# Batched matrix product on one core: loads by groups of four batches, row tiles, and the transposition of x on VectorE

## The chip, the cores and the metric

The kernel runs on one core of a Trainium2 chip. Its time is device microseconds for one launch, here the median of three runs. The profile beside it is one execution of the same program. Five engines work in parallel, each through its own list of instructions in order: TensorE (PE, with its weight loads listed as PEld), VectorE (DVE), ScalarE (ACT), GpSimd (POOL) and SyncE (SP). SP issues the transfers (DMAs) between HBM and the on-chip memory SBUF; 16 DMA engines carry them out. TensorE writes its products to PSUM, a memory of 8 banks, and VectorE or ScalarE copies them from there to SBUF.

## What is computed

```python
batch, dim_i, dim_j, dim_k = 32, 256, 512, 384
# x: (32, 256, 512) float32, y: (32, 512, 384) float32
def reference(x, y):
    return np.einsum('bij,bjk->bik', x, y).astype(np.float32)
```

These are 32 independent products of a 256 x 512 matrix with a 512 x 384 matrix. x is 16.8 MB, y 25.2 MB, the result 12.6 MB: 54.5 MB in all. TensorE needs the summed index j on the partitions for both operands. y has it there as it lies; x must be transposed. Both kernels round x and y to float16 before the products.

## The kernel before

**Tiles.** P is 128, the number of partitions. x is loaded for a group of Q = 4 batches at once (L63): 32 partitions belong to each batch and each holds 8 whole rows of x, 16 KB in one piece. y is loaded for each batch (L69): partition q holds the 4 rows of y with j = 4q to 4q + 3, 6 KB in one piece. The result of a batch is stored (L135) with two rows of 384 on each partition, 3 KB in one piece.

**Steps of the work on one group or batch.** `transpose(q)` turns the x of a group on TensorE: 32 transposes of 128 x 128 float32 elements against an identity matrix (L84), four to a PSUM bank; each full bank is copied out by VectorE (L92) or ScalarE (L94) in turn, rounded to float16 and written with a step of four elements, so that the rows of a batch stand in the order in which they are wanted. `round_y(b)` casts the four 384-element parts of a batch's y, two on ScalarE (L102) and two on VectorE (L104). `multiply(b)` makes the product of a batch from 8 matmuls (L115): four slices t of j, two halves e of the result's rows, each with 128 rows to sum over and 384 columns, gathered in two PSUM banks. `collect(b)` copies the two banks to SBUF, one on ScalarE (L128), one on VectorE (L130).

**Order.** The order on each engine is the order of the program (`keep`). The loop runs over batches s from 0 to B + 1 (L141 on): load the y of batch s + 6 and, with the first batch of a group, its x; collect batch s - 2; multiply batch s - 1; transpose the group if s begins one; round the y of batch s; store batch s - 2. All transfers are issued by SP, in this order, and an instruction that waits on SP holds back all behind it. The buffers: three groups of x, ten batches of y, four of rounded y, two groups of transposed x, ten batches of results, four PSUM banks for the transposes and four for the products. Beside what a transfer waits for by its buffers, it waits until the eighth one before it on SP has landed, as eight semaphores are used in turn; this holds for both kernels.

Of the kernel before, what the change touches and what calls it, by code (L numbers as in the profile page):

```python
# [1 line left out]

# [5 lines left out]


MM_DT = mybir.dt.float16  # L10
F32 = mybir.dt.float32
P = 128


Q = 4

LAG = 8

ON_ACT = ()


@with_exitstack
def kernel(
    ctx: ExitStack,
    tc: tile.TileContext,
    x: bass.AP,
    y: bass.AP,
    out: bass.AP,
):
    nc = tc.nc  # L30

    B, I, J = x.shape
    _, _, K = y.shape

    NI = I // P
    NJ = J // P


    R = Q * NI
    PQ = P // Q  # L40

    const_pool = ctx.enter_context(tc.tile_pool(name="const", bufs=1))
    x_pool = ctx.enter_context(tc.tile_pool(name="x_pool", bufs=3))
    y_pool = ctx.enter_context(tc.tile_pool(name="y_pool", bufs=10))
    yr_pool = ctx.enter_context(tc.tile_pool(name="yr_pool", bufs=4))
    xt_pool = ctx.enter_context(tc.tile_pool(name="xt_pool", bufs=2))
    o_pool = ctx.enter_context(tc.tile_pool(name="o_pool", bufs=10))
    tpsum_pool = ctx.enter_context(tc.tile_pool(name="tpsum", bufs=4, space=bass.MemoryType.PSUM))
    opsum_pool = ctx.enter_context(tc.tile_pool(name="opsum", bufs=4, space=bass.MemoryType.PSUM))


    keep = tc.keep_in_program_order

    identity = const_pool.tile([P, P], F32)
    make_identity(nc, identity)

    x_of, y_of, yr_of, xt_of, ps_of, o_of = {}, {}, {}, {}, {}, {}

    def load(b):
        if b % Q == 0:  # L60
            x_of[b // Q] = x_pool.tile([P, R, J], F32, name="x_sb")
            keep(
                nc.sync.dma_start(  # L63
                    out=x_of[b // Q],
                    in_=x[b : b + Q].rearrange("g (p r) j -> (g p) r j", r=R),
                )
            )
        y_of[b] = y_pool.tile([P, NJ, K], F32, name="y_sb")
        keep(nc.sync.dma_start(out=y_of[b], in_=y[b].rearrange("(q t) k -> q t k", q=P)))  # L69

    def transpose(q):

        x_sb = x_of.pop(q)
        xt_of[q] = xt_pool.tile([P, Q, NJ, NI, PQ, Q], MM_DT, name="xt_sb")
        n = 0
        for t in range(NJ):
            for e in range(NI):  # L80
                t_ps = tpsum_pool.tile([P, Q, Q, PQ], F32, name="t_ps")
                for h in range(Q):
                    keep(
                        nc.tensor.transpose(  # L84
                            t_ps[:, h].rearrange("c g p -> c (g p)"),
                            x_sb[:, h * NI + e, t::NJ],
                            identity,
                        )
                    )
                dst = xt_of[q][:, :, t, e].rearrange("c g p h -> c h g p")  # L90
                if n % 2 == 0:
                    keep(nc.vector.tensor_copy(dst, t_ps))  # L92
                else:
                    keep(nc.scalar.copy(dst, t_ps))  # L94
                n += 1

    def round_y(b):
        y_sb = y_of.pop(b)
        yr_of[b] = yr_pool.tile([P, NJ, K], MM_DT, name="y_r")
        for t in range(NJ):  # L100
            if t % 2 == 0:
                keep(nc.scalar.copy(yr_of[b][:, t], y_sb[:, t]))  # L102
            else:
                keep(nc.vector.tensor_copy(yr_of[b][:, t], y_sb[:, t]))  # L104

    def multiply(b):
        xt_sb, y_r = xt_of[b // Q][:, b % Q], yr_of.pop(b)
        ps_of[b] = [
            opsum_pool.tile([P, K], F32, name=f"o_ps_{e}", tag="o_ps")
            for e in range(NI)  # L110
        ]
        for t in range(NJ):
            for e in range(NI):
                keep(
                    nc.tensor.matmul(  # L115
                        ps_of[b][e],
                        xt_sb[:, t, e].rearrange("c p h -> c (p h)"),
                        y_r[:, t],
                        start=(t == 0),
                        stop=(t == NJ - 1),  # L120
                    )
                )

    def collect(b):
        o_of[b] = o_pool.tile([P, NI, K], F32, name="o_sb")
        for e in range(NI):
            if e % 2 == 0:
                keep(nc.scalar.copy(o_of[b][:, e], ps_of[b][e]))  # L128
            else:
                keep(nc.vector.tensor_copy(o_of[b][:, e], ps_of[b][e]))  # L130
        del ps_of[b]

    def store(b):
        eng = nc.scalar if b in ON_ACT else nc.sync
        keep(eng.dma_start(out=out[b].rearrange("(m e) k -> m e k", m=P), in_=o_of.pop(b)))  # L135


    ahead = LAG - 2
    for b in range(ahead):
        load(b)  # L140
    for s in range(B + 2):  # L141
        if s + ahead < B:
            load(s + ahead)
        if s >= 2:
            collect(s - 2)
        if 1 <= s <= B:
            multiply(s - 1)
        if s < B and s % Q == 0:
            transpose(s // Q)
        if s < B:  # L150
            round_y(s)
        if s >= 2:
            store(s - 2)


# [1 line left out]
_INS = ['x', 'y']  # L157
_OUTS = [((32, 256, 384), 'float32')]


# [23 lines left out]
```

## Time and profile before

| | |
|---|---|
| time, median of 3 runs | 136.32 us (136.06 to 136.57) |
| the profiled execution | 136.52 us |
| its span, first instruction to last | 134.7 us |
| mean granted clock of TensorE in it | 0.887 of full speed |
| read from HBM, written to it | 41.94 MB, 12.58 MB |
| mean rate over the span | 405 GB/s |
| first x landed, first transpose | 8.69 us |
| last eviction (L130) begins | 129.00 us |

The profile page counts the busy time of each engine, cuts the span into 40 slices and gives for each the busy tenths of every engine and of the DMA engines, follows back the chain of work that ended last, and lists groups of like instructions with the time of one and the idle time before them. A group's row reads: line, engine, operation, output and inputs with their shapes, count; busy time in us and the mean of one in ns; the idle time before them and what ended it. Busy shares are means over the whole span, and an engine's idle time costs nothing if it isn't on that chain.

### The profile page before, as it was taken

How to read it: one execution, taken by the hardware profiler on the slowest of the kernel's cores; microseconds unless marked ns; L12 is line 12 of the kernel's file. 1: busy time of each engine (PE TensorE's matmuls, PEld its weight loads, DVE VectorE, ACT ScalarE, POOL GpSimd, SP SyncE). 2: the span in 40 equal slices, each digit the busy share in tenths (PEclk: the TensorE clock that was granted, in tenths of full speed). 3: DMA queues.
4: the chain of work that ended last, by engine and by line, in shares of the span. 5: the costliest groups of instructions: out<-in, count | busy, mean ns of one | idle time of the engine just before them, and what ended most of it. 6: DMA issues, size and time to landing. Idle time of an engine off the chain costs nothing.

```text
span 134.7 us, 1539 instructions
## 1 busy us (share of the span) xinstructions
PE 89.5 (66%) x512; PEld 66.6 (49%) x512; DVE 73.7 (55%) x128; ACT 80.1 (59%) x129; POOL 0.7 (1%) x6
## 2 busy tenths in 40 slices
PE   0049499769677908949794983949459492794920
PEld 0048368644564408925492543936259360793510
DVE  0008855975397503873489340796228870378720
ACT  3007994996299602795479650699218990179910
POOL 2000000000000000000000000000000000000000
PEclk9999999999999985686999599599995999559995
DMA  5999999999999999999999999999999999999992
GB/s 131 399 413 423 447 412 416 416 434 414 404 422 451 425 399 424 421 435 437 400 416 430 438 425 410 421 418 454 407 409 425 433 440 402 421 421 413 412 410 84
DMA packets 10375, 54.62 MB, mean 405 GB/s; under 512 B 1152, under 2 KB 1152, under 8 KB 9344
## 3 DMA queue, kind: packets, MB, share of 16 engines
q1 hardware_dynamic: 10368, 54.53, 97.9%
q8 instruction: 4, 0.07, 0.2%
q14 instruction: 3, 0.02, 0.0%
HBM read 41.94 MB, written 12.58 MB: 405 GB/s over the span
## 4 chain that ended last, share of the span: by engine, by line
DMA 79%; PE 8%; ACT 5%; DVE 2%; issue 2%; SPq 1%; DVEq 0%
DMA y_sb<-in_y_dram 30%; DMA x_sb<-in_x_dram 27%; DMA out_dram<-o_sb 21%; PE o_ps L115 4%; PE t_ps L84 4%; ACT xt_sb L94 2%; ACT y_r L102 2%; DVE xt_sb L92 1%; DVE y_r L104 1%; DVE o_sb L130 0%; SPq L69 0%; ACT o_sb L128 0%; SPq L63 0%; DVEq L130 0%
## 5 line engine op out<-in xcount | busy, mean ns | idle before, releaser
L94 ACT CAST xt_sb<-t_ps 128x512 f16<-128x512 f32 x32 | 39.8, 1350 | 44.0 <-PE t_ps L84 43.9
L92 DVE CAST xt_sb<-t_ps 128x512 f16<-128x512 f32 x32 | 40.1, 1323 | 40.3 <-PE t_ps L84 40.2
L84 PE MATMUL t_ps<-identity,x_sb 128*128 128x128 f32 x256 | 43.4, 340 | 24.5 <-DMA x_sb<-in_x_dram 24.3
L115 PE MATMUL o_ps<-y_r,xt_sb 128*128 128x384 f16 x256 | 46.3, 342 | 14.9 <-ACT y_r L102 14.9
L84 PEld LDWEIGHTS t_ps<-identity,x_sb 128*128 128x128 f32 x256 | 41.1, 216 | 27.8 <-issue 26.4
L115 PEld LDWEIGHTS <-xt_sb 128*128 128x128 f16 x256 | 26.2, 102 | 34.2 <-issue 19.9
L102 ACT CAST y_r<-y_sb 128x384 f16<-128x384 f32 x64 | 30.2, 527 | 0.6 <-DMA y_sb<-in_y_dram 0.6
L130 DVE COPY o_sb<-o_ps 128x384 f32<-128x384 f32 x32 | 17.8, 556 | 15.1 <-PE o_ps L115 15.1
L104 DVE CAST y_r<-y_sb 128x384 f16<-128x384 f32 x64 | 19.9, 354 | 0.4 <-DMA y_sb<-in_y_dram 0.4
L128 ACT COPY o_sb<-o_ps 128x384 f32<-128x384 f32 x32 | 15.4, 483 | 3.8 <-PE o_ps L115 3.8
L94 ACT ACT_TABLE_LOAD x1 | 1.3, 1283 | 0.7 <-PEq L168 0.7
masks.py:199 POOL TENSOR_SCALAR_AFFINE_SELECT identity<-identity 128x128 f32<-128x128 f32 x1 | 0.3, 294 | 0.1
masks.py:197 POOL MEMSET identity<- 128x128 f32 x1 | 0.2, 205 | 0.3 <-POOLq L168 0.3
L168 POOL MEMSET const-bfloat16-1.0<- 128x1 bf16 x1 | 0.1, 102 | 0.0
L168 POOL MEMSET const-uint8-127<- 128x1 uint8 x1 | 0.1, 102 | 0.0
L168 POOL MEMSET const-float32-0.0<- 128x1 f32 x1 | 0.1, 99 | 0.2 <-issue 0.2
L168 POOL MEMSET const-float32-1.0<- 128x1 f32 x1 | 0.1, 99 | 0.0
## 6 DMA issues: line engine op xcount, KB each, us to landing
y_sb<-in_y_dram SPq DMA_DIRECT2D x32, 768.0 KB, 15.1
x_sb<-in_x_dram SPq DMA_DIRECT2D x8, 2048.0 KB, 14.2
out_dram<-o_sb SPq DMA_DIRECT2D x32, 384.0 KB, 14.1
```

The costliest lines, as they stand in the source:

```text
L84: nc.tensor.transpose(t_ps[:, h].rearrange("c g p -> c (g p)"), x_sb[:, h * NI + e, t::NJ], identity,)
L92: keep(nc.vector.tensor_copy(dst, t_ps))
L94: keep(nc.scalar.copy(dst, t_ps))
L102: keep(nc.scalar.copy(yr_of[b][:, t], y_sb[:, t]))
L104: keep(nc.vector.tensor_copy(yr_of[b][:, t], y_sb[:, t]))
L115: nc.tensor.matmul(ps_of[b][e], xt_sb[:, t, e].rearrange("c p h -> c (p h)"), y_r[:, t], start=(t == 0), stop=(t == NJ - 1),)
L128: keep(nc.scalar.copy(o_of[b][:, e], ps_of[b][e]))
L130: keep(nc.vector.tensor_copy(o_of[b][:, e], ps_of[b][e]))
L168: nc = _bacc.Bacc("TRN2", target_bir_lowering=False, num_devices=1)
```

## The change

The kernel now works on groups of four batches throughout, with 32 partitions to each batch in x and in y.

- **Loads.** x as before, one transfer for a group, but into two buffers instead of three. y is loaded for a group too: each of the 32 partitions of a batch holds 16 rows of y, 24 KB in one piece (two buffers). Only the last group's y comes in two halves of 12 KB.
- **Transposition of x.** TensorE no longer transposes and the identity matrix is gone. ScalarE copies x, rounded to float16, into a buffer `xr` so that two rows of x stand side by side as one 4-byte word; it reads with a step of 16 elements and writes with a step of two. VectorE then transposes blocks of 32 x 32 such words within each group of 32 partitions and writes the words with a step of two. A group takes four copies of 1024 elements and four transposes of 512 words.
- **Products.** Each matmul sums over 32 rows instead of 128. The four batches of a group take the four row tiles of TensorE (partitions 0 to 31, 32 to 63 and so on), one after the other in the program. A group has 16 x 2 x 4 = 128 matmuls of 384 columns into all eight PSUM banks.
- **Rounding of y.** Eight parts of 768 elements in a group: five on VectorE and three on ScalarE (`ROUND`).
- **Order.** In step n: load the x of group n + 2 and the y of group n + 1, round y and multiply group n, transpose the x of group n + 1, collect group n, store group n - 1. The last step stores group 7.

The core of the diff:

```diff
+LATE = 8
+LAST = 2
+ROUND = (1, 0, 1, 1, 0, 1, 0, 1)
...
+    S = P // Q
+    R = I // S
+    C = J // S
...
+    NE = I // P
+    A = R // NE // 2
+    N = B // Q
...
+    x_pool = ctx.enter_context(tc.tile_pool(name="x_pool", bufs=2))
+    xr_pool = ctx.enter_context(tc.tile_pool(name="xr_pool", bufs=1))
     xt_pool = ctx.enter_context(tc.tile_pool(name="xt_pool", bufs=2))
+    y_pool = ctx.enter_context(tc.tile_pool(name="y_pool", bufs=2))
+    yr_pool = ctx.enter_context(tc.tile_pool(name="yr_pool", bufs=2))
+    o_pool = ctx.enter_context(tc.tile_pool(name="o_pool", bufs=12))
+    psum_pool = ctx.enter_context(tc.tile_pool(name="psum", bufs=Q * NE, space=bass.MemoryType.PSUM))
...
+    def load_y(n):
+        y_of[n] = y_pool.tile([P, C, K], F32, name="y_sb")
+        src = y[n * Q : (n + 1) * Q].rearrange("g (p c) k -> (g p) c k", c=C)
+        w = C // (LAST if n == N - 1 else 1)
+        for c in range(0, C, w):
+            keep(nc.sync.dma_start(out=y_of[n][:, c : c + w], in_=src[:, c : c + w]))
...
+    def transpose_x(n):
+        x_sb = x_of.pop(n)
+        xr = xr_pool.tile([P, A, NE, C, S], F32, name="x_r")
+        xt = xt_pool.tile([P, C, NE, S, A], F32, name="xt_sb")
+        for a in range(A):
+            for e in range(NE):
+                keep(
+                    nc.scalar.copy(
+                        xr[:, a, e].bitcast(MM_DT).rearrange("q c (j w) -> q w c j", w=2),
+                        x_sb[:, a * 2 * NE + e : (a + 1) * 2 * NE : NE].rearrange(
+                            "q w (j c) -> q w c j", c=C
+                        ),
+                    )
+                )
+                keep(nc.vector.transpose(xt[:, :, e, :, a], xr[:, a, e]))
+        xt_of[n] = xt
...
+    def round_y(n):
...
+        w = C // len(ROUND)
+        for k, dve in enumerate(ROUND):
+            part = slice(k * w, (k + 1) * w)
+            if dve:
+                keep(nc.vector.tensor_copy(y_r[:, part], y_sb[:, part]))
+            else:
+                keep(nc.scalar.copy(y_r[:, part], y_sb[:, part]))
...
+    def multiply(n, y_r):
+        xt_sb = xt_of.pop(n)
+        ps = [[psum_pool.tile([P, K], F32, name="o_ps") for e in range(NE)] for g in range(Q)]
+        for c in range(C):
+            for e in range(NE):
+                for g in range(Q):
+                    rows = slice(g * S, (g + 1) * S)
                     keep(
+                        nc.tensor.matmul(
+                            ps[g][e],
+                            xt_sb[rows, c, e].rearrange("q p a -> q (p a)").bitcast(MM_DT),
+                            y_r[rows, c],
+                            start=(c == 0),
+                            stop=(c == C - 1),
                         )
                     )
...
+    load_x(0)
+    load_x(1)
+    load_y(0)
+    transpose_x(0)
+    for n in range(N + 1):
+        if n + 2 < N:
+            load_x(n + 2)
+        if n + 1 < N:
+            load_y(n + 1)
+        if n < N:
+            ps = multiply(n, round_y(n))
+        if n + 1 < N:
+            transpose_x(n + 1)
+        if n < N:
+            collect(n, ps)
+        for b in range(max((n + 1) * Q - LATE, 0), min((n + 2) * Q - LATE, B) if n < N else B):
+            store(b)
```

The code of `collect` and `store` is as before, but `collect` takes a whole group: four evictions on ScalarE and four on VectorE.

## The prediction

> **What bounds the kernel now.** I read the page from the top. Parts 1 to 3 first:
>
> ```profile
> PE 89.5 (66%) x512; PEld 66.6 (49%) x512; DVE 73.7 (55%) x128; ACT 80.1 (59%) x129; POOL 0.7 (1%) x6
> DMA  5999999999999999999999999999999999999992
> GB/s 131 399 413 423 447 412 416 416 434 414 404 422 451 425 399 424 421 435 437 400 416 430 438 425 410 421 418 454 407 409 425 433 440 402 421 421 413 412 410 84
> q1 hardware_dynamic: 10368, 54.53, 97.9%
> ```
>
> No engine is busy for more than 66% of the span, while the DMA row has a 9 in every slice but the first and the last. Queue q1 took 97.9% of 134.7 us, which is 131.9 us; the other 2.8 us lie at the two ends. Then the chain of waits (part 4), and the windows of the last microseconds:
>
> ```profile
> DMA 79%; PE 8%; ACT 5%; DVE 2%; issue 2%; SPq 1%; DVEq 0%
> ```
> ```profile
> 125.00:131.00 6.00, 3.97 (x25) 2.16 (x23) 3.31 (x8) 3.50 (x9) 0.00 (x0) 1.00 1.03 412
> 131.00:132.00 1.00, 0.00 (x0) 0.00 (x0) 0.00 (x0) 0.00 (x0) 0.00 (x0) 0.74 0.77 307
> 132.00:133.00 1.00, 0.00 (x0) 0.00 (x0) 0.00 (x0) 0.00 (x0) 0.00 (x0) 0.50 0.29 117
> 133.00:134.70 1.70, 0.00 (x0) 0.00 (x0) 0.00 (x0) 0.00 (x0) 0.00 (x0) 0.50 0.02 7
> ```
>
> The last two columns are the DMA share and GB/s. Until 131 us the transfers run at full rate, though the last load of y has landed by 122.5 us: stores of earlier batches fill the time in which the last batches are rounded, multiplied and copied out. So the kernel is bound by its transfers from end to end. To be faster it needs cheaper transfers; it gets slower as soon as the transfers have to wait. Last, the groups of part 5, as prices:
>
> ```profile
> L94 ACT CAST xt_sb<-t_ps 128x512 f16<-128x512 f32 x32 | 39.8, 1350 | 44.0 <-PE t_ps L84 43.9
> L92 DVE CAST xt_sb<-t_ps 128x512 f16<-128x512 f32 x32 | 40.1, 1323 | 40.3 <-PE t_ps L84 40.2
> L115 PE MATMUL o_ps<-y_r,xt_sb 128*128 128x384 f16 x256 | 46.3, 342 | 14.9 <-ACT y_r L102 14.9
> L102 ACT CAST y_r<-y_sb 128x384 f16<-128x384 f32 x64 | 30.2, 527 | 0.6 <-DMA y_sb<-in_y_dram 0.6
> L104 DVE CAST y_r<-y_sb 128x384 f16<-128x384 f32 x64 | 19.9, 354 | 0.4 <-DMA y_sb<-in_y_dram 0.4
> L130 DVE COPY o_sb<-o_ps 128x384 f32<-128x384 f32 x32 | 17.8, 556 | 15.1 <-PE o_ps L115 15.1
> L128 ACT COPY o_sb<-o_ps 128x384 f32<-128x384 f32 x32 | 15.4, 483 | 3.8 <-PE o_ps L115 3.8
> ```
>
> The first two rows matter most. 512 elements cost 1.32 us there on either engine; at the rate of the last row (384 in 0.48 us, no gaps in what it writes) they would cost about 0.6. What sets them apart is that they write two-byte elements 8 bytes apart: about 2.3 ns for each element.
>
> [...] The trace has no row tiles, but the clock does fall to 0.50 there after a pause of 4 us.[...]
>
> **The change part by part.**
>
> *Transfers.* The bytes stay. The trace's packets take 121 ns for 3 KB (stores), 234 for 6 KB (y) and 611 for 16 KB (x), a straight line. It gives 913 ns for the new 24 KB packets of y, against 4 x 234 = 936, and 460 for the 12 KB ones of the last group. Each of the 16 engines had 32 x 8 packets of y with a mean of 235 ns, 60.3 us; it gets 56 of 913 and 16 of 460, 58.5 us. Saved: 1.8 us. Floor of the span: 134.7 - 1.8 = 132.9 us, if the transfers never wait. Data then flows from 0.9 to 131.0. A group (x 4.9, y 7.3, stores 3.9) takes 16.1 us.
>
> *ScalarE, for each group of four batches.* Three roundings of 768 elements: two 384-element casts in a row took 0.93 to 0.99 us, so 0.84 for one (less one fixed cost), 2.5 us. Four copies of x into the interleaved buffer, 1024 elements each, then four evictions of 0.48. The copies are the largest unknown: they read at steps of 64 bytes[...] and write two-byte elements 4 bytes apart.[...] Upper end: the 2.3 ns of the nearest row, 2.5 us; it isn't a strict bound, since reads at such steps do not occur before. I take 2.0 us[...]. Sum: 2.5 + 8.0 + 1.9 = 12.4 us, below 16.1, so in the middle of the run it is hidden by the transfers.
>
> *VectorE.* Five roundings of 0.6 (two casts of 384 in a row took 0.62), four transposes of 512 words, four evictions of 0.56. A transpose:[...] 1.3 by the row that writes 8 bytes apart, as it does; I take 1.0. Sum 9.2 us. The transposes follow the copies one by one, so only the last adds to a path.
>
> *TensorE.* 256 transposes go (43.4 us, at no gain in time: they lay beside transfers). The 256 products become 1024 of 32 rows. In before, 32 products in a row took 5.36 us, 161 ns from one to the next, 384 columns. Perfect overlap of four tiles gives 40 ns each, none gives 161. I take 50 at full clock (128 x 50 = 6.4 us a group) and 8.3 us where the burst starts at half clock[...]. Both are below 16.1. The identity and its build go; POOL had it ready at 1.3 us, x landed at 8.7: nothing.
>
> *Start.* x0, x1 and y0 keep the DMA busy until 0.9 + 0.9 (slow first packets) + 4.9 + 4.9 + 7.3 = 18.9 us. x2 waits on SP until ScalarE has read x0: 8.7 + 8.0 = 16.7, data 1.5 us after issue (my estimate from the start, where the full rate comes 2.3 us after the first issue): no gap. Behind it y1 needs nothing. x3 waits for the copies of x1, which ScalarE runs after the roundings of y0: 19.9 + 2.5 + 8.0 = 30.4, data at 31.9, and the DMA runs out at 31.1: a gap of 0.8 us, with y2 and the first stores queued behind x3 on SP. Later groups have slack, 12.4 against 16.1.
>
> *End.* Here nothing is left to hide behind. After y6's packets 22.9 us of transfers remain: y7 7.4, four groups of stores 15.5. So y6 is in at 108.1 and seen at 109.1 us. Products of group 6: 109.1 + 0.65 (first rounding) + 8.3 = 118.0. But the evictions stand behind the copies of x7: 109.1 + 2.5 + 8.0 = 119.6, last transpose 120.6, four evictions 122.8. All eight PSUM banks belong to one group, and the roundings of y7 stand behind these evictions too (y7 itself is seen at 116.7 and 120.4). First rounding 123.4, products of group 7, after a pause of over 5 us, 8.3: 131.7. First eviction and issue 132.4, data 133.9. The stores of group 6 had been issued in time and kept the DMA busy to 127.2, so it idles 6.7 us. Four stores 3.9, then 1.9 as now: 139.7 us. With the 0.8 at the start 140.5. Before, one batch stood between the last load and the end; now it is four, and the four before them.
>
> Outside the span lay 1.8 us (136.52 - 134.7), and the profiled run is 0.2 above the median: 140.5 + 1.8 - 0.2 = 142.1 us against 136.32. Forecast: slower, 142 us.
>
> **Rivals.**
>
> *B, cheap copies.* At 1.05 us the evictions of group 6 wait only for the products: 118.0, done 120.3, rounding 120.9, products at full clock[...] 127.3, issue 128.0, data 129.5: idle 2.3 us. Span 135.2, time 136.8. For it: no row reads at such steps, so nothing proves a penalty. Against: the 1.32 us rows.
>
> *C, faster.* Copies under about 1.3 us and, decisive, TensorE never at half clock and at no more than 50 ns a product: group 6 ends at 116.2, its evictions at 118.4, group 7 at 125.4, data at 127.6. The idle time shrinks to 0.4 us and the cheaper packets win: span 133.3, time 134.9. It turns where both product bursts and the evictions between them together need less than about 17 us. Against: pauses of some 8 us before each burst.
>
> *D, tiles in series.* Products 161 ns apart: 20.7 us a group, 23.5 with evictions and rounding, so TensorE is the bound: 20.5 + 8 x 20.7 + 7 x 2.8, plus 8 for the stores, 214 us, time about 215.[...]
>
> *E, dear copies.* At 3.3 us ScalarE needs 13.2 + 2.5 + 1.9 = 17.6 a group, more than the transfers: 21.9 + 7 x 17.6 + 17, about 162, time 163.
>
> With copies at 2.5 the forecast's sum gives gaps of 2.8 at the start, 144.5 in all, time 146.
>
> **How the numbers follow.** Forecast (copies between 1.5 and 2.8 us, or products at up to 80 ns) 0.53, own range 138 to 150; B 0.20; C 0.09; D 0.08; E 0.10. About 0.5% is what a measurement of this kernel tells from none: 135.6 to 137.0. C is faster; B's 136.8 sits at the edge, 0.11 of it same and 0.09 slower; the rest is slower: 0.80. The range goes from C's 135 to 155, which takes in the lower part of E and leaves out D, the rest of E and the lower half of C.
>
> **What would show it.** Right: y in 24 KB packets of some 913 ns; the ScalarE copy line at about 2 us; the DMA row at 9 until some 127 us and then a hole before the last four stores; half clock at the start of the bursts; products 40 to 60 ns apart. Wrong: a copy near 1 us (B or C), products over 100 ns apart (D), ScalarE busy over 90% (E), holes in the middle of the DMA row, or no hole at the end.

## The result: slower, by a hole before the last stores (profile after)

The changed kernel takes 140.94 us (median of 4 runs, 139.79 to 141.5) against 136.27 us, the median of four runs of the kernel before (the table above has the first three): 1.033 times as long (95% interval 1.0261 to 1.0398). The forecast was 142 us, slower. The profiled execution is the shortest of the four, 139.79 us with a span of 138.0; the others had spans of 139.0, 139.3 and 139.7. The mean granted clock fell from 0.887 to 0.791.

The page of the changed kernel: busy times, the clock, DMA and GB/s rows in 40 slices of 3.45 us, the queue, and the shares of the chain of waits.

```profile
PE 60.1 (44%) x1024; PEld 31.4 (23%) x1024; DVE 57.0 (41%) x104; ACT 90.6 (66%) x89; POOL 0.2 (0%) x4
...
PEclk9999999997579758965896558965589655995995
DMA  4999999999999999999999899999999999999256
GB/s 119 423 437 465 442 394 437 461 418 356 444 427 348 394 456 432 425 405 427 438 461 427 346 448 450 434 394 415 443 439 432 392 418 440 415 401 393 97 216 240
...
q1 hardware_dynamic: 7056, 54.53, 95.1%
...
DMA 67%; ACT 19%; PE 5%; issue 2%; DVE 2%; DVEq 1%; SPq 0%; ACTq 0%
```

The DMA row is full to slice 37 and then drops to 2 and 5 where the kernel before had a 9 to the last slice but one. The queue took 95.1% of 138.0, 131.2 us, where it had taken 131.9: 0.7 us less of work on it, in a span 3.3 us longer. ScalarE's share of the chain of waits went from 5% to 19%: it now sets when the end begins. The windows show the hole itself (columns: window, length, busy time and count of PE, PEld, DVE, ACT, POOL, granted clock, DMA share, GB/s):

```profile
127.00:128.00 1.00, 1.00 (x16) 0.50 (x12) 0.00 (x0) 0.00 (x0) 0.00 (x0) 0.50 0.92 366
128.00:129.00 1.00, 1.00 (x28) 0.65 (x24) 0.00 (x0) 0.00 (x0) 0.00 (x0) 0.91 0.44 175
129.00:130.00 1.00, 1.00 (x32) 0.65 (x28) 0.00 (x0) 0.00 (x0) 0.00 (x0) 1.00 0.20 69
130.00:131.00 1.00, 1.00 (x32) 0.53 (x23) 0.00 (x0) 0.00 (x0) 0.00 (x0) 1.00 0.00 0
131.00:132.00 1.00, 0.21 (x8) 0.00 (x0) 0.76 (x2) 0.93 (x3) 0.00 (x0) 1.00 0.00 0
132.00:133.00 1.00, 0.00 (x0) 0.00 (x0) 1.00 (x3) 0.70 (x2) 0.00 (x0) 1.00 0.33 129
133.00:134.00 1.00, 0.00 (x0) 0.00 (x0) 0.19 (x1) 0.00 (x0) 0.00 (x0) 1.00 0.99 393
```

What the DMA share lacks of 1 in the first six rows adds up to 0.08 + 0.56 + 0.80 + 1 + 1 + 0.67 = 4.1 us. Until 131 us TensorE is alone at work in it: group 7 is multiplied while nothing is left to store. What leads up to it stands in the timeline from 111 us on (start and duration in us, engine, line and operation, in brackets the idle time before it and what ended that):

```profile
111.38 2.30 ACT L108 CAST y_r<-y_sb 128x768 f16<-128x768 f32 x3 [4.79 <-DMA y_sb<-in_y_dram]
...
112.07 8.24 PE L120 MATMUL o_ps<-y_r,xt_sb 32*128 32x384 f16 x128 [8.25 <-DVE y_r L106]
113.58 7.47 ACT L89 CAST x_r<-x_sb 128x1024 f16<-128x1024 f32 x4
...
120.93 1.61 ACT L135 COPY o_sb<-o_ps 128x384 f32<-128x384 f32 x4
121.08 0.71 DVE L96 STREAM_TRANSPOSE xt_sb<-x_r 128x512 f32<-128x512 f32 x1 [1.13 <-ACT x_r L89]
121.72 1.91 DVE L137 COPY o_sb<-o_ps 128x384 f32<-128x384 f32 x4
...
124.15 7.06 PE L120 MATMUL o_ps<-y_r,xt_sb 32*128 32x384 f16 x128 [3.84 <-DVE y_r L106]
131.07 1.63 ACT L135 COPY o_sb<-o_ps 128x384 f32<-128x384 f32 x4 [6.33 <-PE o_ps L120]
```

y6 is seen at 111.4. ScalarE rounds its parts, copies x7 four times, and comes to the evictions of group 6 at 120.93 without an idle moment; VectorE follows at 121.72 after the last transpose. The products of group 6 had ended at 120.3. Group 7 is multiplied from 124.15 to 131.2. From y6 seen to group 7 started: 12.8 us. The groups of the page give the prices (busy time, mean ns of one | idle before):

```profile
L120 PE MATMUL o_ps<-y_r,xt_sb 32*128 32x384 f16 x1024 | 60.1, 406 | 71.1 <-DVE y_r L106 71.1
L89 ACT CAST x_r<-x_sb 128x1024 f16<-128x1024 f32 x32 | 59.6, 1936 | 6.3 <-DMA x_sb<-in_x_dram 6.3
L96 DVE STREAM_TRANSPOSE xt_sb<-x_r 128x512 f32<-128x512 f32 x32 | 22.8, 713 | 49.1 <-ACT x_r L89 49.1
L108 ACT CAST y_r<-y_sb 128x768 f16<-128x768 f32 x24 | 18.4, 833 | 28.7 <-DMA y_sb<-in_y_dram 28.7
L106 DVE CAST y_r<-y_sb 128x768 f16<-128x768 f32 x40 | 19.5, 554 | 21.8 <-DMA y_sb<-in_y_dram 21.8
```

One copy of x takes 1.94 us, one transpose 0.71. A matmul is listed with 406 ns, yet the bursts of 128 take 6.72 to 8.24 us, 53 to 64 ns for each: four row tiles are at work at once, so here the count over the burst has to be read and not the mean.

Last, the transfers in full flow, where no engine holds them up. Before, in two windows, and from the start to 120 us:

```profile
34.00:50.00 16.00, 10.06 (x64) 7.12 (x64) 8.99 (x16) 9.60 (x16) 0.00 (x0) 0.99 1.02 422
50.00:120.00 70.00, 51.48 (x278) 39.14 (x279) 39.65 (x67) 41.85 (x66) 0.00 (x0) 0.82 1.02 423
0.00:120.00 120.00, 82.28 (x470) 61.87 (x471) 66.51 (x114) 72.01 (x114) 0.70 (x6) 0.89 1.00 414
```

And after:

```profile
34.00:50.00 16.00, 9.76 (x156) 4.88 (x160) 9.40 (x18) 13.66 (x15) 0.00 (x0) 0.71 1.01 412
50.00:120.00 70.00, 35.35 (x620) 18.14 (x612) 30.64 (x55) 50.60 (x48) 0.00 (x0) 0.71 1.01 424
0.00:120.00 120.00, 52.75 (x896) 27.44 (x896) 50.17 (x90) 84.23 (x78) 0.20 (x4) 0.79 0.99 414
```

For 70 us both move the same 423 to 424 GB/s, and over the first 120 us both have the mean of 414: the whole of the lost time comes after 120 us. The packets are longer as forecast (24 KB: median 912 ns, mean 928; 12 KB: 460), and four of the old ones lasted 4 x 235 = 940, but the rate didn't rise: before, the DMA share was 1.02 there, so by the profile its packets overlapped a little more.

### The profile page after: what moved, and what is told of

The parts are those of the page before. It is cut to its first block, busy times and chain, and to the rows that moved or that the text cites. A ratio compares the mean times of both kernels' runs of the same rounds, so it can differ in the third digit from the quotient of the medians.

```text
span 138.0 us, 2433 instructions
## 1 busy us (share of the span) xinstructions
PE 60.1 (44%) x1024; PEld 31.4 (23%) x1024; DVE 57.0 (41%) x104; ACT 90.6 (66%) x89; POOL 0.2 (0%) x4
## 3 DMA queue, kind: packets, MB, share of 16 engines
q1 hardware_dynamic: 7056, 54.53, 95.1%
## 4 chain that ended last, share of the span: by engine, by line
DMA 67%; ACT 19%; PE 5%; issue 2%; DVE 2%; DVEq 1%; SPq 0%; ACTq 0%
DMA out_dram<-o_sb 49%; ACT x_r L89 15%; DMA y_sb<-in_y_dram 13%; DMA x_sb<-in_x_dram 5%; PE o_ps L120 5%; ACT y_r L108 2%; ACT o_sb L135 2%; DVE o_sb L137 1%; DVEq L185 1%; DVE y_r L106 0%; SPq L65 0%; SPq L140 0%; DVEq L137 0%; ACTq L135 0%
## 5 line engine op out<-in xcount | busy, mean ns | idle before, releaser
L120 PE MATMUL o_ps<-y_r,xt_sb 32*128 32x384 f16 x1024 | 60.1, 406 | 71.1 <-DVE y_r L106 71.1
L89 ACT CAST x_r<-x_sb 128x1024 f16<-128x1024 f32 x32 | 59.6, 1936 | 6.3 <-DMA x_sb<-in_x_dram 6.3
L120 PEld LDWEIGHTS <-xt_sb 32*128 32x128 f16 x1024 | 31.4, 115 | 99.5 <-DVE y_r L106 52.6
L96 DVE STREAM_TRANSPOSE xt_sb<-x_r 128x512 f32<-128x512 f32 x32 | 22.8, 713 | 49.1 <-ACT x_r L89 49.1
L108 ACT CAST y_r<-y_sb 128x768 f16<-128x768 f32 x24 | 18.4, 833 | 28.7 <-DMA y_sb<-in_y_dram 28.7
L106 DVE CAST y_r<-y_sb 128x768 f16<-128x768 f32 x40 | 19.5, 554 | 21.8 <-DMA y_sb<-in_y_dram 21.8
L137 DVE COPY o_sb<-o_ps 128x384 f32<-128x384 f32 x32 | 15.3, 538 | 5.3 <-PE o_ps L120 5.3
L135 ACT COPY o_sb<-o_ps 128x384 f32<-128x384 f32 x32 | 12.8, 483 | 6.3 <-PE o_ps L120 6.3
```

Of the source, the lines that this page charges most:

```text
L89: nc.scalar.copy(xr[:, a, e].bitcast(MM_DT).rearrange("q c (j w) -> q w c j", w=2), x_sb[:, a * 2 * NE + e : (a + 1) * 2 * NE : NE].rearrange(
L96: keep(nc.vector.transpose(xt[:, :, e, :, a], xr[:, a, e]))
L106: keep(nc.vector.tensor_copy(y_r[:, part], y_sb[:, part]))
L108: keep(nc.scalar.copy(y_r[:, part], y_sb[:, part]))
L120: nc.tensor.matmul(ps[g][e], xt_sb[rows, c, e].rearrange("q p a -> q (p a)").bitcast(MM_DT), y_r[rows, c], start=(c == 0), stop=(c == C - 1),)
L135: keep(nc.scalar.copy(o_sb[:, e], ps[g][e]))
```

## The experiments

Theory T: the time lost is the hole, and its length is set by the chain from y6's landing to the first store of group 7 (roundings, copies of x7, evictions of 6, products of 7) against the stores queued behind y7. Rivals: the products of group 6 at half clock, granted 0.50 from 111 to 117 us in after (R1), or the landing of y7 (R2), hold that chain rather than the copies; the transfers themselves became slower (R3). The expectations, recorded run by run, number their rivals in their own way. The table has, from the one profile of each, when y6 is seen, when group 7 is multiplied, and the hole (what the DMA shares in the 1-us windows from 127 us to the return of full rate lack of 1).

| kernel | median, us | ratio to before (95%) | y6 seen | products of 7 | hole |
|---|---|---|---|---|---|
| after | 140.94 | 1.033 (1.0261 to 1.0398) | 111.4 | 124.15 to 131.2 | 4.1 |
| e1_copies_split | 137.5 | 1.0103 (1.0073 to 1.0132) | 111.8 | 122.52 to 129.6 | 2.9 |
| e4_read_dense | 137.15 | 1.006 (1.004 to 1.0081) | 111.9 | 122.13 to 129.2 | 2.3 |
| e5_write_dense | 141.46 (one run) | | 111.9 | 124.59 to 132.9 | 5.6 |
| e2_y7_first | 140.74 | 1.0317 (1.0278 to 1.0355) | 112.4 | 125.14 to 132.7 | 5.2 |
| e3_stores_late | 139.39 | 1.0232 (1.0217 to 1.0247) | 109.4 | 122.18 to 130.0 | 1.3 |
| e10_hold_stores | 137.49 | 1.0079 (1.0048 to 1.0111) | 108.5 | 121.30 to 129.0 | 1.7 |
| e8_split_emajor | 136.84 | 1.004 (1.0029 to 1.0052) | 111.5 | 122.08 to 127.7 | 1.0 |
| e6_split_slices | 137.53 | 1.0103 (1.0063 to 1.0144) | in slices | 120.19 to 127.3 | 0.1 |
| e9_split_warm | 138.17 | 1.0146 (1.0129 to 1.0162) | 111.8 | 121.63 to 128.7 | 2.0 |
| e11_split_warm32 | 137.74 | 1.0125 (1.0088 to 1.0162) | 112.8 | 121.94 to 128.9 | 1.9 |
| e13_split_emajor_warm_y7 | 138.0 | 1.0132 (1.0115 to 1.015) | 112.8 | 121.87 to 128.9 | 1.8 |
| e12_split_emajor_hold | 136.65 | 1.0031 (1.0016 to 1.0045) | 107.8 | 117.54 to 123.9 | none |

### The copies of x on the path

**e1** takes half of the copies out of the end: the first half of x of group n + 1 is copied and transposed ahead of the roundings of group n, in a time in which ScalarE waits for y anyway.

```diff
+        if n + 1 < N:
+            transpose_x(n + 1, (0,))
         if n < N:
             ps = multiply(n, round_y(n))
         if n + 1 < N:
-            transpose_x(n + 1)
+            transpose_x(n + 1, (1,))
```

> Edit: two of the four copies of x (and their transposes) of the next group run ahead of the roundings of y, in the pause in which ScalarE waits for y; the other two stay behind them. The span's loss is a hole of about 4 us (127.6 to 132.5 us) in the transfers before the last four stores. Theory: the chain to those stores runs from y6's landing through two paths of nearly the same length, the copies of x7 (evictions of group 6 begin at 120.9 on ScalarE, 121.7 on VectorE) and the products at half clock (end 120.3). With the copies out of the way the evictions wait for the products alone: about 1 us earlier, the start's gap of about 0.5 us goes too, so 139 to 140 us instead of 140.9. Rival 1, the copies alone set the chain: evictions 3.7 us earlier, 137 us or less. Rival 2, the copies have no part in it: no change, 140.9.

The timeline of e1, the same stretch as above (the copy is line 90 here):

```profile
112.43 7.58 PE L120 MATMUL o_ps<-y_r,xt_sb 32*128 32x384 f16 x128 [8.92 <-DVE y_r L106]
114.02 3.77 ACT L90 CAST x_r<-x_sb 128x1024 f16<-128x1024 f32 x2
...
119.88 1.63 ACT L135 COPY o_sb<-o_ps 128x384 f32<-128x384 f32 x4 [2.10 <-PE o_ps L120]
120.05 1.95 DVE L137 COPY o_sb<-o_ps 128x384 f32<-128x384 f32 x4 [1.51 <-PE o_ps L120]
...
122.52 7.06 PE L120 MATMUL o_ps<-y_r,xt_sb 32*128 32x384 f16 x128 [2.51 <-DVE y_r L106]
```

Two copies are left in this stretch, and both evictions now wait for PE: the copies no longer hold them. Group 7 starts 1.6 us earlier and the median falls by 3.4 us. By the profiles the expected chain holds: the evictions begin 1.0 us earlier, and the hole shrinks by 1.2 us. The medians show more, since the profiled execution of after is the shortest of its runs and that of e1 the longest; why the other runs of after are longer is open. By its median e1 lies outside what was expected, near the rival in which the copies alone set the chain; by its profile the products of group 6, granted 0.50 up to 117.0 us, now come last.

**e4** and **e5** alter the copy's order of elements, the one on the read side, the other on the write side, and leave its place. Both then multiply other elements than the task asks for, as many and in the same shapes.

```diff
 # e4, the source of the copy
-                            "q w (j c) -> q w c j", c=C
+                            "q w (c j) -> q w c j", c=C
 # e5, its destination
-    .rearrange("q c (j w) -> q w c j", w=2)
+    .rearrange("q c (w j) -> q w c j", w=2)
```

> Edit: ScalarE's copy of x reads 32 neighbouring elements instead of elements 64 bytes apart; it writes as before (so the words hold other elements of x, and the products are others). The copy takes 1.94 us for 1024 elements[...]. Theory: the reads at 64 bytes cost the extra, so the copy falls to about 1.05 us and the time by about 1 us as in the split of the copies. Rival 5, the two-byte writes at 4 bytes cost it: the copy stays at 1.94 us.

> Edit: ScalarE's copy of x writes 32 neighbouring float16 elements instead of elements 4 bytes apart, and reads at 64-byte steps as before (the words then hold other pairs, so the products are others). Theory after the dense read (copy fell from 1.94 to 1.24 us): most of the extra comes from the reads, a part from the writes; here the copy stays at 1.7 to 1.9 us. Rival 5, reads and writes wait for each other and the slower one counts: the copy stays at 1.94 us.

The groups, the copy's row of e4:

```profile
L89 ACT CAST x_r<-x_sb 128x1024 f16<-128x1024 f32 x32 | 39.4, 1328 | 6.5 <-DMA x_sb<-in_x_dram 6.5
```

and of e5:

```profile
L89 ACT CAST x_r<-x_sb 128x1024 f16<-128x1024 f32 x32 | 59.0, 1916 | 6.3 <-DMA x_sb<-in_x_dram 6.3
```

Dense reads take 0.61 us off a copy (1936 to 1328 ns), dense writes 0.02. So the price that can be taken off singly lies in reading one float32 in every 64 bytes: 0.6 ns an element. The 1.05 us expected of e4 was the author's estimate; no row shows it. e5 came out just above the 1.7 to 1.9 us expected and near its rival, that the slower side alone counts; a copy dense on both sides wasn't run, so whether the writes hold the remaining 1.33 us is open. With the four copies in 4.94 instead of 7.47 us, e4's group 7 starts at 122.13 and its median is 3.8 us below after's, though every other part of the kernel is the same. Two ways of shortening the same stretch gave 3.4 and 3.8 us by the medians, and holes of 2.9 and 2.3 us for 4.1: T holds. R3 has room only for what is left, 0.9 us in e4, whose loads and stores are those of after, and the equal 414 GB/s up to 120 us speak against it too.

### The landing of y7

**e2** issues the load of y7 one step earlier, ahead of four stores.

```diff
-        if n + 1 < N:
+        if n + 1 < N - 1:
             load_y(n + 1)
...
+        if n == N - 3:
+            load_y(N - 1)
         for b in range(max((n + 1) * Q - LATE, 0), min((n + 2) * Q - LATE, B) if n < N else B):
```

> Edit: the two loads of y7 are issued ahead of the stores of group 4 instead of behind them, so y7 lands about 3.9 us earlier and y6 as before. Theory: the products of group 7 wait for the evictions of group 6, that is for y6, and not for y7; the same transfers lie ahead of the hole, so the time stays at 140.9 within 0.7 us. Rival 3, the late landing of y7 sets the end: about 3 us less, 138 us.

140.74 us: no change from 140.94. R2 falls for the kernel as changed. The timeline of e2 shows what holds group 7 instead:

```profile
113.07 6.82 PE L120 MATMUL o_ps<-y_r,xt_sb 32*128 32x384 f16 x128 [8.01 <-DVE y_r L106]
...
121.94 1.61 ACT L135 COPY o_sb<-o_ps 128x384 f32<-128x384 f32 x4
...
122.71 1.91 DVE L137 COPY o_sb<-o_ps 128x384 f32<-128x384 f32 x4
...
125.14 7.60 PE L120 MATMUL o_ps<-y_r,xt_sb 32*128 32x384 f16 x128 [5.25 <-DVE y_r L106]
```

The products of group 6 end at 119.9, two microseconds before ScalarE comes to the first eviction. R1 falls too while all four copies stand there.

### The stores behind the last load

The other side of the hole is how much there is to store behind y7. **e3** lets every group's stores wait one step longer; **e10** does so from step 4 on only, so that the start is left as it was.

```diff
 # e3
-LATE = 8
+LATE = 12
-    o_pool = ctx.enter_context(tc.tile_pool(name="o_pool", bufs=12))
+    o_pool = ctx.enter_context(tc.tile_pool(name="o_pool", bufs=16))
 # e10, o_pool as in e3, HOLD = 4
-        for b in range(max((n + 1) * Q - LATE, 0), min((n + 2) * Q - LATE, B) if n < N else B):
+        due = n if n < HOLD else n - 1 if n < N else N
+        for b in range(stored * Q, due * Q):
             store(b)
+        stored = due
```

> Edit: each group's stores are issued one step later (LATE 12 instead of 8), with 16 result buffers instead of 12; all loads move ahead of one more group of stores. Theory: y6 and y7 land 3.9 us earlier and 3.9 us more of stores lie behind them, so the hole before the last stores closes nearly wholly: 137 us (the floor of the transfers, 131.2 us of busy queue and 2.8 at the ends plus 1.8 outside the span, is 135.8). Rival 4, the loss lies in the stream of transfers itself (larger loads, two buffers for x and y in place of three and ten): the time stays near 140.9, with the lost time spread over the run.

> Edit: the kernel after the change, but the stores are held back by one more step only from step 4 on (16 result buffers), so the stores of group 3 and of all later ones go behind the loads of the next group. The stores held back from the first step on (139.4 us) had brought y6 only 2.1 us earlier instead of 3.9, as the transfers stalled between 30 and 60 us, where no stores were left to cover the late loads of x. Theory: without those stalls y6 comes 3.5 to 3.9 us earlier, as much more of stores lies behind it, and the hole closes: 137.0 us. Rival 4, the loss lies in the stream: 139.4 us or more, as in the run before.

In both y6 is seen 2 to 3 us earlier, as four stores fewer stand ahead of it, and those 3.9 us of stores go behind y7 instead. e3 gives most of it back: its rates are 356 GB/s in 30 to 34 us, 398 in 34 to 50 and 417 in 50 to 120, against 393, 412 and 424 in after; on these stretches that is about 0.4, 0.5 and 1.2 us; why, I didn't follow up. e10 has 367, 406 and 424; as its program up to step 4 is that of after, but for four more result buffers, the first two show how far two executions of the same start can differ. Its timeline:

```profile
108.54 2.30 ACT L108 CAST y_r<-y_sb 128x768 f16<-128x768 f32 x3 [1.01 <-DMA y_sb<-in_y_dram]
...
118.10 1.60 ACT L135 COPY o_sb<-o_ps 128x384 f32<-128x384 f32 x4
...
121.30 7.73 PE L120 MATMUL o_ps<-y_r,xt_sb 32*128 32x384 f16 x128 [5.12 <-DVE y_r L106]
```

Its hole is 1.7 us and its median 3.5 us below after's, with all four copies still on the path: 12.8 us from y6 seen to group 7 started, as in after. So the hole can be narrowed from either side.

### The products at the end

**e8** is e1 with the halves e outermost in the products, and evictions by halves, so that half of the banks are copied out while the other half is still multiplied.

```diff
-        for c in range(C):
-            for e in range(NE):
+        for e in range(NE):
+            for c in range(C):
                 for g in range(Q):
...
-        for g in range(Q):
-            for e in range(NE):
-                if e % 2 == 0:
+        for e in range(NE):
+            for g in range(Q):
+                if g % 2 == 0:
```

> Edit: the split of the copies as before; the products of a group make one half of the rows of all four batches first, then the other, and the evictions follow in that order, two of each half on ScalarE and two on VectorE. Theory: half of the evictions of group 6 lie beside its products, so those of group 7 start 0.5 to 1 us earlier: 136.8 us against 137.5. Rival 2 (evictions and roundings are not on the chain): 137.5 us.

136.84 us (17 runs), 0.7 us below e1. The timeline of e8 shows more than the overlap of the evictions:

```profile
112.15 8.32 PE L120 MATMUL o_ps<-y_r,xt_sb 32*128 32x384 f16 x128 [8.21 <-DVE y_r L106]
...
122.08 5.61 PE L120 MATMUL o_ps<-y_r,xt_sb 32*128 32x384 f16 x128 [1.61 <-ACT y_r L108]
```

The pause before group 7 is 1.61 us, and the burst runs at full clock throughout (1.00 in each window from 122 to 128 us), 5.61 us. In e1 the pause was 2.51 us, the clock fell to 0.50 at 123.8 us, and the burst took 7.06. Group 7 starts 0.4 us earlier than in e1 and ends 1.9 us earlier, so by the profiles most of the gain is the clock's. Whether the shorter pause saved it isn't shown: the length of a pause alone doesn't decide that (see the last section).

**e6** is e1 with every y in four slices of 6 KB a partition (`w = C // 4`), so that the products can start on the first slice.

> Edit: the split of the copies as before, and the y of every group comes in four loads with a quarter of the rows of each batch (6 KB in one piece instead of 24). Theory: the products can follow the loads slice by slice, so those of group 6 end about 3 us after y6 has landed instead of 8, the evictions and the products of group 7 start about 2.5 us earlier, and the hole closes; the queue pays 0.7 us for the smaller packets (234 ns for 6 KB against 912 for 24): 136.3 us. Rival 7, one load for four batches costs nothing, only the order of the work does: 138 us, the packets' 0.7 more than the split alone.

137.53 us, as e1. The hole is gone (372 and 407 GB/s in 128 to 130 and 130 to 132 us), but the rate up to 120 us was 411 GB/s on average against 415 in e1, some 1.2 us. The queue's packets took 132.9 us (97.4% of 136.4) for e1's 130.9. So within the changed kernel the longer packets do look cheaper, by about what their times add up to, while the kernel before moves its 6 KB pieces at 414 GB/s over the same 120 us. Whether the pieces or the order of loads and stores make the difference isn't settled.

**e9**, **e11** and **e13** try R1 with an instrument: products whose results are overwritten fill TensorE's pause, so that group 6 starts at full clock. e9 puts 56 of them ahead of each group on e1, e11 puts 128; e13 is e11 with e2's early y7 and e8's order of halves.

```diff
+        if 0 < n < N - 1:
+            for c in range(14):
+                for g in range(Q):
+                    rows = slice(g * S, (g + 1) * S)
+                    keep(nc.tensor.matmul(ps[g][0], ..., yr_of[n - 1][rows, c], start=True, stop=True))
```

> Edit: the split of the copies as before, and ahead of the products of groups 1 to 6 there are 56 more products on old data into the same PSUM banks (the real products start afresh there), which fill the pause of TensorE before y lands. Theory: half clock makes the products of group 6 last 7 to 8 us instead of 5.3; warm, they end at 117.7, the evictions then wait for the copies (118), the products of group 7 start 2 us earlier at full clock, and the hole nearly closes: 136.0 us against 137.5 of the split alone, and 5.3 to 5.6 us for the products of group 6. Rival 6, the clock has no part in the end: 137.5 us.

> Edit: the split of the copies, and ahead of the products of groups 1 to 6 128 more products on old data (instead of 56, which were over 4.5 us before the real ones, so that the clock had fallen again). Theory: the pause is filled to about 1 us, the products of group 6 take 5.3 us instead of 7 to 8, those of group 7 start at about 121 us; they are then held for y7's second half (seen at 122.9 to 123.8 us) and end at about 128: 136.3 us against 137.5. Rival 6, the clock has no part in the end: 137.5 to 138.2 us as with 56.

> Edit: split of the copies, products by halves of the rows, y7 ahead of the stores of group 4, and the 128 products that fill TensorE's pause. Theory: with the clock kept up the evictions of group 6 end near 119 us, and with y7 seen at 119 nothing holds the products of group 7, which end near 125 us while the stores of group 6 last to 127.5: no hole, 135.8 us. Rival 6 (no part of the clock): 136.8 us.

In e9 the instrument failed: the 56 ran from 104.7 to 107.9, then 4.5 us went by before y6 came, and group 6 took 6.71 us, where e11's took 5.38 with the clock at 1.00. With 128 it worked. The timeline of e11 (the products of the kernel are line 136 here):

```profile
113.45 5.38 PE L136 MATMUL o_ps<-y_r,xt_sb 32*128 32x384 f16 x128 [1.55 <-DVE y_r L106]
...
118.74 1.59 ACT L151 COPY o_sb<-o_ps 128x384 f32<-128x384 f32 x4
...
121.94 6.98 PE L136 MATMUL o_ps<-y_r,xt_sb 32*128 32x384 f16 x128 [3.10 <-DVE y_r L106]
...
123.89 1.56 ACT L108 CAST y_r<-y_sb 128x768 f16<-128x768 f32 x2 [2.80 <-DMA y_sb<-in_y_dram]
```

Group 6 takes 5.38 us at a clock of 1.00 instead of e1's 7.58, and from y6 seen to group 7 started it is 9.1 us for e1's 10.7: the chain is 1.6 us shorter, and the hole 1.9 for 2.9. Yet the time is no lower, 137.74 us. y6 is seen 1 us later than in e1, which I can't explain, and time less hole is 0.8 us more than in e1: the instrument goes with a loss elsewhere. ScalarE goes from the copies to the evictions without a pause, so the copies are last again, and the second half of y7 is seen only at 123.89. e13 moves y7's load as well and stays at 138.0, with y6 at the same late 112.8; its group 7 starts no earlier (121.87) and takes 7.06 us at half clock for a part (0.74 in 122 to 124 us, 0.50 in 124 to 126). So the copies and half clock in group 6 are two limits that lie within a microsecond or two of each other; taking one away shows the other. That y7's landing comes next isn't shown.

### All that helped, together

**e12** is e1 with e8's order and e10's stores.

> Edit: split of the copies, products by halves of the rows, and the stores held back from step 4 on. Theory: everything of the last two groups comes 3.9 us earlier against the stores, so no hole is left; the time falls from 136.8 to the floor of the transfers, 131.0 us of busy queue and 4.6 around it: 135.6 us, 0.5% below the kernel before. Rival 4 (what is left of the loss lies in the stream): 136.8 us.

The windows of e12 (columns as above):

```profile
128.00:129.00 1.00, 0.00 (x0) 0.00 (x0) 0.00 (x0) 0.00 (x0) 0.00 (x0) 0.50 1.03 408
129.00:130.00 1.00, 0.00 (x0) 0.00 (x0) 0.00 (x0) 0.00 (x0) 0.00 (x0) 0.50 1.02 409
130.00:131.00 1.00, 0.00 (x0) 0.00 (x0) 0.00 (x0) 0.00 (x0) 0.00 (x0) 0.50 0.92 369
131.00:132.00 1.00, 0.00 (x0) 0.00 (x0) 0.00 (x0) 0.00 (x0) 0.00 (x0) 0.50 0.63 252
```

No hole: the engines are done by 125 us and the stores flow on to the end, as in the kernel before. Yet 136.65 us (8 runs) is 1.0031 times the kernel before (1.0016 to 1.0045). Expected were 135.6; the rival, that the rest lies in the stream, had 136.8. The start isn't to blame: from 0 to 50 us e12 moves 404 GB/s on average and the kernel before 401, to 120 us 415 and 414. The packets took 130.8 us of its queue (97.0% of 134.8), 1.1 us less than before, and the span is the same, 134.8 for 134.7. So the floor of the loads and stores as changed isn't lower than the old one by anything like the forecast saving. No version here beat the kernel before.

A sum over the profiled executions: time less hole is 139.79 - 4.1 = 135.7 for after, 138.24 - 2.9 = 135.3 for e1, 136.6 - 1.0 = 135.6 for e8 and 137.62 - 1.7 = 135.9 for e10; e2, e4, e5, e9, e11 and e13 leave 135.4 to 136.2. So over ten kernels with holes of 1.0 to 5.6 us the hole accounts for the differences to 0.9 us. (e3 and e6 leave 138.1 and 138.2: they are the two with the lowest mean rate up to 120 us, 408 and 411 GB/s.) The kernel before (136.52) and e12 (136.6) have no hole and lie 0.3 to 1.3 us above the ten: with stores to the end the 16 engines finish unevenly (0.92 and 0.63 in the last rows above), and part of what I count as hole is probably that same uneven finish, met earlier.

## Why the prediction was right, and which terms were off

The mechanism and its place were right: a hole before the last four stores, made by the chain y6, copies of x7, evictions of 6, products of 7. e1, e4 and e10 show it from both sides. That the time came so near is in part luck: a hole forecast too long by 2.6 us stands against a saving of 1.8 us that didn't come. The sizes:

- **Transfers, the term that was mis-sized.** 1.8 us were to be saved by longer packets. The packets have the durations forecast (912 ns and 460 in the median), but the rate in full flow is the same, and e12, which has no hole, ends no earlier than before. Half of the 1.8 us goes already in the sum: the old packets entered with their mean (235 ns), the new ones with the 913 of a straight line, which came out as their median; with their mean of 928 the sum gives 0.9 us. For the rest, the times of single packets were added up as if the engines worked on one after the other; with shares of 1.01 and 1.02 they overlap, and a little more so with the small packets of the kernel before. Why they do so there isn't settled: e6, with small packets in the new order, is slower. The effect is seen at y6: forecast at 109.1, or 109.9 with the 0.8 us of the start, and seen at 111.4, 1.5 us late, where some 7/8 of the 1.8 us should have been won.
- **Start.** x2 was issued at 15.8 us (forecast 16.7) and x3 at 30.2 (30.4). Transfers were slower there: 393 GB/s in 30 to 34 us against 422 in e1, where x1 is copied earlier and x3 is issued at 26.7, which is 0.3 us for the 0.8 forecast (e2 and e10, whose start is that of after, have 379 and 367). In 34 to 50 us they were slower than before as well (412 against 422), but that stays in e1 and e12 (412, 414), so it isn't the wait of x3 on the copies that I named; its cause is open, and over the first 50 us after and before have the same 401 GB/s.
- **Copies, 2.0 us.** Measured 1.94, and the reads at 64-byte steps are the dear part, as supposed (1.94 to 1.33 us in e4).
- **Other steps of the chain.** From y6 seen to group 7 started 12.8 us for 14.3: copies 7.5 for 8.0, last transpose 0.71 for 1.0 (it writes at a step of 8 bytes, as the copies of 512 elements out of PSUM did before in 1.32 us; what the step adds here wasn't measured), four evictions 1.9 for 2.2, ScalarE's roundings 2.2 for 2.5 until the copies begin, first rounding 0.5 for 0.6.
- **Products.** 8.24 us for group 6 (8.3) and 7.06 for group 7 (8.3). The burst of e11 at full clock gives 5.38 / 128 = 42 ns a product where 50 was taken, the author's estimate: 3.8 of them in the 161 ns of one product before.
- **Sum.** The first store of group 7 was issued at about 131.9 for 133.2 (132.4 and the 0.8 of the start): 1.5 us late by the transfers, 2.8 early by the chain. Its data was back in flow 0.8 us after issue for 1.5, and the end took 5.3 us for 5.8. So the span is 138.0 for 140.5 and the hole 4.1 for 6.7; here too errors of both signs partly cancelled. The other three executions were 1.0 to 1.7 us longer, which leaves the median within 1.1 us of the forecast. Those three have no profile; whether y6's landing or the clock makes that difference is open.

The rivals: D and E fall by the products' spacing of 53 to 64 ns and ScalarE's 66%. B's case, cheap copies (1.05 us each, the author's estimate), is nearly what e4 built: 1.33 us a copy and 137.15 us, where B had 136.8. But B counted on full clock for group 7, and e4's group 7 took 7.04 us after a pause of 2.86 (a mean clock of 0.61 in 124 to 126 us). C needed the transfers to be cheaper, and they weren't.

## What to carry to other kernels

In a kernel bound by its transfers, add up what lies between the last load and the last store, and set it against the transfers queued behind that load: a larger group for each step lengthens the first and has to be paid for with stores held back. Take a transfer's price from the rate in full flow, in the order of loads and stores in which it will run, and not from the times of its packets. And where several limits end within a microsecond or two, as the copies and half clock did here, removing one is worth only the distance to the next.

## What the runs showed of the hardware

- With four row tiles of 32 rows and 384 columns a product ends every 42 ns (e11's burst at full clock, 128 in 5.38 us), weight loads included, against 161 ns for the 128-row products before: four in 168 ns.
- A VectorE transpose of 512 four-byte words on 128 partitions takes 0.71 us, with its writes 8 bytes apart.
- The clock fell to 0.50 with pauses of 2.51 us (e1), 2.86 (e4) and 3.10 (e11) before the burst, 1.3 us into the burst in e1. The length of a pause alone doesn't decide. In e13 a burst took 5.38 us, the time of e11's at full clock, after 2.27. The kernel before has both outcomes after 1.9 us, with a mean clock of 0.76 in the first burst and 1.00 in the second:

```profile
73.52 6.99 PE L115 MATMUL o_ps<-y_r,xt_sb 128*128 128x384 f16 x32 [1.86 <-ACT y_r L102]
...
90.64 5.36 PE L115 MATMUL o_ps<-y_r,xt_sb 128*128 128x384 f16 x32 [1.89 <-ACT y_r L102]
```

In e1 the clock rose at 117.0, fell at 123.8 and rose at 127.2 us, 6.8 and 3.4 us apart, by the means of its 1-us windows (0.53 in 116 to 117, 0.89 in 123 to 124, 0.91 in 127 to 128). What decides isn't shown by these runs.
